# Splitting work moved behind the PSUM reads of each slot, the last output columns in two groups, and TensorE operands at multiples of 256 bytes

## The chip, the core and the metric

The kernel runs on one core of one Trainium2 chip. The metric is the device time of one launch in microseconds (us): the median of three runs is 1772.46 us (1771.05 to 1772.84). TensorE (PE) multiplies, VectorE (DVE) and ScalarE (ACT) work on rows in SBUF and read results out of PSUM, GpSimd (POOL) does small copies and powers, and SyncE (SP) issues all DMAs of this kernel in program order.

## The reference, cut to what matters

One layer of a streaming encoder over 2048 prompt tokens and 64 sample tokens of width 1024, all in float32:

```python
h = rmsnorm(x, norm_in_w) * (1 + scale[:, None]) + shift[:, None]
proj = h @ w_in                         # 1024 -> 7184 columns
b_gate, c_gate, h_a, g_a, z, xbc_raw, dt_raw = jnp.split(proj, idx, axis=-1)
conv_u, new_a = causal_dwconv(c_gate * h_a, buf_a, conv_a_w)
y_a = gated_rmsnorm(b_gate * conv_u, g_a, norm_a_w)
xbc, new_b = causal_dwconv(xbc_raw, buf_b, conv_b_w)   # then + bias, silu
y, s_new = ssd_chunked(xs, dt, a, bs, cs, s0)          # chunked scan, 16 heads, state 128
y_b = gated_rmsnorm(y + d_skip * xs, z, norm_b_w)
out = jnp.concatenate([y_a, y_b], axis=-1) @ w_out     # 2048 -> 1024
return rmsnorm(x + gate[:, None] * out, norm_f_w), new_a, new_b, s_new
```

The outputs are the normalised rows of both sequences and the final states of the two convolutions and of the scan.

## The kernel before, in words

**Split operands.** Every float32 factor of the large products is split into a rounded part `hi` (fp32r) and a rest `lo`, and a product is the sum of three: hi·hi, hi·lo, lo·hi. ACT writes `hi` (a cast), DVE writes `lo` (a subtraction that reads `hi`).

**Projection, `phase_project`.** The tokens go through in two passes: pass 0 takes tokens 0 to 1023, pass 1 tokens 1024 to 2047 and the 64 sample tokens (`PASS`, line 22). The 1024 token columns (1088 in pass 1) and the 1024 rows of the weights are cut in halves, and the four half products of a pair of output tiles are made with seven products (`PRODS`, line 23: A11, S1, S2, S4, S3, A12, A22) in the manner of Strassen and Winograd; S1 to S4 are sums and differences of quarters of `h`. A *group* `g` is one pair of output tiles (256 weight columns), and a *slot* `(g, s)` is one of its seven products: 12 matmuls of 512 columns in pass 0, 24 matmuls of 272 columns in pass 1 (two halves `u` of 12). Groups 0 and 1 are plain products; groups 2 to 27 are pass 0, 28 to 54 pass 1, and 55 is a plain last pair.

**Order inside a slot** (lines 1229 to 1256). Each engine executes its instructions in the order in which they are written: the product on PE (`product`, L276); work put off from the slot before (`run_later`); the weight `hi` of a coming product on ACT (`w_hi`, L242); the *hooks* of that slot; background DVE work (`run_bg`); the weight `lo` on DVE (`w_lo`, L233, with the subtractions that make the Strassen sums of the weights); the read of PSUM (`evac`): for s = 0, 1, 2 an ACT copy into `keep` (L301), for s = 3, 4, 5 a DVE addition (L309), for s = 6 an ACT copy (L307); then the entries of `behind`. Later products accumulate in the same PSUM bank as earlier ones, so slot 2 waits for the read of slot 0, slot 3 for that of slot 1, slot 4 for that of slot 2, slot 6 for that of slot 4, and the first slots of pass 1 for the banks of group 27.

**Between the passes.** The normalised `h` of pass 1 is made during groups 18 to 23 and stored in HBM (`hs_d`). `sums_in(i)` (two calls, for two row halves) loads four quarters into rows 2 to 5; `sums_step(i, n)` (four per call, L849, DVE) makes one of the sums in place and stores it to `hq_d` (L850). They are hooks: `sums_in(0)` in slot (23,6) and its steps in (24,2) to (24,5); `sums_in(1)` in (24,5) and its steps in (25,1) to (25,4). Then `second_in(j, r)` loads the quarter or sum for product `j` into two rows, and `second(j)` splits it into the operand that pass 1 reads: two ACT casts (L171) and two DVE subtractions (L172) of 1088 columns, then the load for `j + 3`. `second(0)`, `(1)`, `(4)`, `(5)`, `(6)` are hooks of slots (27,1), (27,2), (27,6), (28,0), (28,2); `second(2)` and `(3)` stand in `behind` at (27,4) and (27,5).

**Mixing, `phase_mix`.** Sixteen chunks of 128 tokens (and the 64 sample tokens first) go through the scan, both gated norms and the output projection. `out_mm` makes 512 output columns with 24 matmuls (L1430, L1437); `take_b` (L1452 to L1455) scales, multiplies by the gate, adds the residual row on DVE, and sums squares on ACT; `end_rms` makes the factor of the final norm; `scale_out` (L1466) multiplies 1024 columns and stores the row (L1467). For all chunks but the last, the second half of this runs during the next chunk.

**Addresses.** Tiles of a pool are laid one behind the other, each rounded up to 32 bytes per partition; `const`, `stats`, `lp` (later `sp`) are stacked upwards, `hs1`, `hs2`, `hs3` (later `sp1`, `wop`) downwards from the end at 229,344 = 895·256 + 224 bytes. Adding up the sizes: the weights `w0` to `w6` and all operands `hi`, `lo` start 96 bytes past a multiple of 256; `woh`, `wol`, `vah`, `vbh`, `xb` and `state` start 224 past one. In pass 1 a row block of an operand has 2176 bytes, so block k odd starts 128 further, and the half u = 1 another 1088 further. The one exception is group 0 and 1's second token half, `a21`, whose parts lie in row tiles at 160, 192 (hi) and 32, 64 (lo) past a multiple of 256.

Of the kernel before, what the change touches and what calls it, by code (L numbers as in the profile page):

```python
# [27 lines left out]
def kernel(  # L28
# [46 lines left out]
    rbs = const.tile([128, 1], F32, tag="rbs", name="rbs")  # L75
    mhalf = const.tile([128, 1], F32, tag="mhalf", name="mhalf")
    stats = pool(ctx, "stats", bufs=4)

    def ca_w(k, t):
        return par[:, k * 8 + t:k * 8 + t + 1]  # L80
# [20 lines left out]
    def phase_project():  # L101
# [75 lines left out]
            h_tile(q, 544)  # L177
        for i in (0, 1, 6, 7, 2, 3, 4, 5):
            row(i, [128, 1094], f"row{i}_")
        raws = [hs1.tile([128, KT, 256], F32, tag=f"raw{i}", name=f"raw{i}") for i in range(2)]  # L180

        def load_rows(chunks, rows):
            out = []
# [655 lines left out]
        def sums_in(i):  # L839
            for n, (k0, o) in enumerate(((0, 0), (0, 544), (4, 0), (4, 544))):  # L840
                t = row(2 + n, [128, 2, 544], "h_q")
                SP.dma_start(out=t, in_=hs_d[:, k0 + 2 * i:k0 + 2 * i + 2, o:o + 544])
                blocks[n] = t

        def sums_step(i, n):
            a11, a21, a12, a22 = (blocks[x] for x in range(4))
            out, x, y, op = ((a22, a21, a22, ALU.add), (a21, a11, a21, ALU.subtract),
                             (a11, a22, a11, ALU.subtract), (a12, a12, a11, ALU.subtract))[n]
            DVE.tensor_tensor(out=out, in0=x, in1=y, op=op)  # L849
            SP.dma_start(out=hq_d[n, :, 2 * i:2 * i + 2, :], in_=out)  # L850

        for i, t0 in enumerate((23 * 7 + 6, 24 * 7 + 5)):
            hook_at(t0, lambda i=i: sums_in(i))
            for n in range(4):
                hook_at(t0 + 3 + n, lambda i=i, n=n: sums_step(i, n))

        tm = {}
        SOURCE = {"A11": (hs_d, 0, 0), "A12": (hs_d, 4, 0), "A22": (hs_d, 4, 544),
# [17 lines left out]
        hook(26, 0, lambda: second_in(0, 6))  # L876
        hook(26, 1, lambda: second_in(1, 2))
        hook(26, 2, lambda: second_in(2, 4))
        behind = {}
        for j, t, late in ((0, 1, 0), (1, 2, 0), (2, 4, 1), (3, 5, 1), (4, 6, 0), (5, 7, 0), (6, 9, 0)):  # L880
            if late:
                behind[27, t] = lambda j=j: second(j)
            else:
                hook_at(27 * 7 + t, lambda j=j: second(j))

        hook(30, 0, lambda: dt_project(1, 2))
        hook(30, 2, lambda: dt_gather(1))
# [263 lines left out]
        def last_pair():  # L1151
# [16 lines left out]
            fast = [p1.tile([128, 8, 128], F32, tag="lt", name="lt", bufs=2) for _ in range(2)]  # L1168
            p1.tile([128, 8, 128], F32, tag="rb", name="rb_")
            xbs = [p1.tile([128, 8, 128], F32, tag="xb", name="xb", bufs=2) for _ in range(2)]  # L1170
            wop = pool(ctx, "wop", side="right", reuse_waits="tile")
            for k in (0, 1, 2, 3, 4, 5, 7, 8, 9, 10, 11, 12, 13, 14, 15, 6):
                wo[k] = (wop.tile([128, D], F32R, tag=f"woh{k}", name=f"woh{k}"),
# [52 lines left out]
        for g in range(2, last):  # L1226
            p = int(g >= NP0)
            slot_us = 2.75 if p == 0 else 3.05
            for s in range(7):
                now[0] = 7 * g + s  # L1230
                open_banks(p, g, s)
                product(p, g, s)
                run_later()
                if s == 1:
                    w_load(g + 2)
                if s == 2:
                    work[g][1]["begin"](p)
                tg, tj = (g, 6) if s == 0 else (g + 1, s - 1)
                if tg < last:
                    w_hi(tg, tj)  # L1240
                for fn in hooks.get((g, s), ()):
                    fn()
                cost = (W_COST[tj] if tg < last else 0.7) + (0.7 if 3 <= s <= 5 else 0.0) + (0.2 if p and s >= 3 else 0.0)
                credit = min(credit + slot_us - cost, slot_us)
                credit = run_bg(credit)
                if tg < last:
                    w_lo(tg, tj)
                elif s > 0:
                    last_w(s - 1)
                evac(p, g, s)  # L1250
                if (g, s) in behind:
                    behind[g, s]()
                if s == 4:
                    work[g][1]["done"](p, 1)
                if s == 6:
                    work[g][1]["done"](p, 0)
# [36 lines left out]
    def phase_mix():  # L1293
# [156 lines left out]
        def take_b(c, nn, t, ps, r, xr, ss):  # L1450
# [3 lines left out]
            DVE.tensor_tensor(out=xr[:n, s], in0=xr[:n, s], in1=t[:n], op=ALU.add)  # L1454
            ACT.activation(out=t[:n], in_=xr[:n, s], func=AF.Square, accum_out=ss[:n, nn:nn + 1])  # L1455

        def end_rms(c, ss):
            n = ntok(c)
            DVE.tensor_tensor(out=ss[:n, 0:1], in0=ss[:n, 0:1], in1=ss[:n, 1:2], op=ALU.add)
            rf = stats.tile([128, 1], F32, tag="rf", name="rf")  # L1460
            rsqrt_mean(ss[:n, 0:1], n, rf[:n])
            return rf
# [78 lines left out]
        for c in range(16):  # L1541
            n, nxt, nx2 = 128, c + 1, c + 2
            more = nxt < 16
            vb = vb_of.pop(c)
            vbh = split_act(vb, n, "vbh")
            if more:
                prefetch(nxt, 1)
                prefetch_z(nxt, 1)
            if pending:
                pending[0]()  # L1550
            if more:
                va = prefetch_va(nxt)
                ssd1(nxt, 0)
            ra = inv_rms(sqa, n, "ra")
            if pending:
                pending[1]()
            split_dve(vb, n, vbh)
            square(vb, n)
            if pending:
                pending[2]()  # L1560
            sqb = sum_sq(vb, n, "vbh")
            if c == 0:
                SP.dma_start(out=gate, in_=g_d[0].partition_broadcast(128))
            if more:
                xr_next = prefetch_x(nxt)
            if not more:
                store_state()
            pa = out_mm(vah, 0, c, 0)
            if more:
                ssd2(nxt, 0)  # L1570
                decay(nxt, 1)
            t0 = take_a(c, pa, ra)
            if more:
                join1(nxt, 0)
                ssd1(nxt, 1)
                join2(nxt, 0)
                if nx2 < 16:
                    prefetch(nx2, 0)
                    prefetch_z(nx2, 0)
            pa = out_mm(vah, 0, c, 1)  # L1580
            rb_ = inv_rms(sqb, n, "rb")
            if more:
                ssd2(nxt, 1)
            t1 = take_a(c, pa, ra)
            if more:
                vah = split_act(va, n, "vah")
                split_dve(va, n, vah)
                square(va, n)
                join1(nxt, 1)
                sqa = sum_sq(va, n, "vah")  # L1590
                join2(nxt, 1)
                if nx2 < 16:
                    decay(nx2, 0)
            ss = stats.tile([128, 2], F32, tag="fs", name="fs", bufs=2)
            pb0 = out_mm(vbh, 8, c, 0)
            take_b(c, 0, t0, pb0, rb_, xr, ss)
            pb1 = out_mm(vbh, 8, c, 1)

            pending = ends(c, t1, pb1, rb_, xr, ss)
            if more:  # L1600
                xr = xr_next
        for f in pending:
            f()
        stack.close()

    with tc.manual_schedule():
# [30 lines left out]
```

## Time and profile before

| | us |
|---|---|
| median of 3 runs | 1772.46 |
| the profiled execution's own time | 1769.35 |
| its span, first to last instruction | 1767.5 |
| PE busy | 1716.4 (97%) |
| DVE busy | 1306.8 (74%) |
| ACT busy | 826.9 (47%) |
| mean granted TensorE clock | 0.993 |

Where the profile is asked for a stretch, times count from the start of the span. Pass 0 of the Strassen groups begins at 86.0 us, group 24 at 523.98, pass 1 at 606.27; the mixing phase begins after 1215 us. "Idle" behind a row is the time for which that engine had nothing to do before the instruction, and the name behind it is what ended it.

### The profile page before, as it was taken

To read this page: it belongs to the slowest core of one execution; us is meant where nothing else is said; L and a number is where in the kernel's file an instruction comes from. 1 tells how busy PE (TensorE), PEld (TensorE's weight loads), DVE (VectorE), ACT (ScalarE), POOL (GpSimd) and SP (SyncE) were. 2 spreads that over 40 slices of the span, in tenths; PEclk is the share of its full clock that TensorE was granted. 3 is DMA by queue.
4 is the path that set the end of the run, shared out by engine and by line. 5 is a ranking of instruction groups with operands and counts; after the bars stand their busy time and mean duration, and the time that the engine had idled before them with its cause. 6 is when DMAs were issued, how large, how long until landed. Compare 5 with 4: busy or idle time off the path is not lost.

```text
span 1767.5 us, 26974 instructions
## 1 busy us (share of the span) xinstructions
PE 1716.4 (97%) x10561; PEld 1512.3 (86%) x10561; DVE 1306.8 (74%) x2019; ACT 826.9 (47%) x1575; POOL 102.5 (6%) x224
## 2 busy tenths in 40 slices
PE   5999999999999999999999999999899999999997
PEld 4788888887887799999999999999588888888886
DVE  5787779766576646678768767646788888888885
ACT  5644344444653645434333443325455555545551
POOL 0000000000000000001001000000011111101011
PEclk9999999999999999999999999999899999999999
DMA  9222323232548742322322242324653343434341
GB/s 338 72 76 92 96 84 102 89 107 86 170 151 287 248 123 61 91 74 76 113 82 73 74 119 79 113 90 143 213 179 139 137 150 125 160 107 169 108 149 36
DMA packets 186722, 220.20 MB, mean 125 GB/s; under 512 B 21300, under 2 KB 152356, under 8 KB 186596
## 3 DMA queue, kind: packets, MB, share of 16 engines
q1 hardware_dynamic: 186596, 218.49, 38.2%
q8 instruction: 83, 1.36, 0.3%
q14 instruction: 43, 0.35, 0.1%
HBM read 164.31 MB, written 54.15 MB: 124 GB/s over the span
## 4 chain that ended last, share of the span: by engine, by line
PE 86%; DVE 5%; DMA 4%; ACT 3%; issue 2%; SPq 0%; POOL 0%; POOLq 0%; DVEq 0%; ACTq 0%
PE bank L276 54%; PE mm L1430 14%; PE mm L1437 7%; PE sd L1355 2%; PE sd L1359 2%; PE sd L1361 2%; PE sd L1327 1%; DMA h_q<-hs_d 1%; PE sd L1331 1%; DMA praw<-in_w_mod_dram 1%; PE bank L1041 1%; DVE w L233 1%; DMA hq_d<-h_q 0%; DMA xt<-in_x_prompt_dram 0%; PE bank L530 0%
## 5 line engine op out<-in xcount | busy, mean ns | idle before, releaser
L276 PE MATMUL bank<-hiS,w 128*128 128x272 f32 (+1 forms) x2560 | 598.8, 323 | 9.6 <-ACT keep L301 9.5
L276 PEld LDWEIGHTS bank<-hiS,w 128*128 128x128 f32 x2560 | 432.4, 189 | 46.4 <-ACT keep L301 13.0
L276 PE MATMUL bank<-hiA,w 128*128 128x272 f32 (+1 forms) x1920 | 448.9, 322 | 5.8 <-DVE z_row L309 2.4
L276 PE MATMUL bank<-loS,w 128*128 128x272 f32 (+1 forms) x1280 | 412.4, 322 | 0.0
L276 PEld LDWEIGHTS bank<-hiA,w 128*128 128x128 f32 x1920 | 322.8, 188 | 34.7 <-DVE z_row L309 3.3
L233 DVE TENSOR_TENSOR w<-raw,w 128x512 fp32r<-128x512 f32 x318 | 217.9, 688 | 160.0 <-ACT w L242 149.0
L242 ACT CAST w<-raw 128x512 fp32r<-128x512 f32 x318 | 196.1, 622 | 256.7 <-PE bank L276 131.2
L276 PE MATMUL bank<-loA,w 128*128 128x272 f32 (+1 forms) x960 | 308.2, 321 | 0.0
L276 PEld LDWEIGHTS bank<-loS,w 128*128 128x128 f32 x1280 | 242.2, 189 | 15.8
L276 PEld LDWEIGHTS bank<-loA,w 128*128 128x128 f32 x960 | 180.5, 188 | 11.9
L301 ACT COPY keep<-bank 128x272 f32<-128x272 f32 (+1 forms) x240 | 105.9, 450 | 130.7 <-PE bank L276 130.2
L382 DVE SCALAR_TENSOR_TENSOR acc<-raw_row,par,acc 128x1024 f32<-128x1024 f32 (+1 forms) x96 | 126.5, 1318 | 2.0
L233 DVE TENSOR_TENSOR raw<-raw 128x512 f32<-128x512 f32 x161 | 111.0, 690 | 3.7
L1430 PE MATMUL mm<-woh,vbh 128*128 128x512 f32 (+1 forms) x272 | 110.0, 404 | 0.0
L1430 PE MATMUL mm<-woh,vah 128*128 128x512 f32 (+1 forms) x272 | 109.4, 402 | 0.0
L1430 PE MATMUL mm<-wol,vbh 128*128 128x512 f32 (+1 forms) x272 | 106.6, 392 | 0.0
L1430 PE MATMUL mm<-wol,vah 128*128 128x512 f32 (+1 forms) x272 | 106.4, 391 | 0.0
L1289 ACT ACTIVATE lt<-rb,acum 128x128 f32<-128x128 f32 x240 | 73.4, 388 | 3.5 <-DMA rb<-r_d 3.1
L242 ACT CAST w<-t 128x512 fp32r<-128x512 f32 x53 | 32.8, 618 | 74.1 <-PE bank L276 74.1
L1437 PE MATMUL mm<-woh,vbh 128*128 128x512 f32 (+1 forms) x272 | 67.2, 389 | 0.0
L1437 PE MATMUL mm<-woh,vah 128*128 128x512 f32 (+1 forms) x272 | 67.2, 389 | 0.0
L1455 ACT ACTIVATE t<-xr 128x512 f32<-128x512 f32 (+1 forms) x34 | 21.5, 633 | 92.9 <-DVE xr L1454 92.9
(282 smaller groups left out, 2381.8 us busy)
## 6 DMA issues: line engine op xcount, KB each, us to landing
raw<-in_w_in_dram SPq DMA_DIRECT2D x56, 1024.0 KB
xb_d<-acc SPq DMA_DIRECT2D x32, 512.0 KB
xb<-xb_d SPq DMA_DIRECT2D x32, 512.0 KB
rb<-r_d SPq DMA_DIRECT2D x30, 512.0 KB
xt<-in_x_prompt_dram SPq DMA_DIRECT2D x16, 512.0 KB
praw<-in_w_mod_dram SPq DMA_DIRECT2D x16, 512.0 KB
z_d<-z_row SPq DMA_DIRECT2D x16, 512.0 KB
va_d<-c_row SPq DMA_DIRECT2D x16, 512.0 KB
```

The source lines that it names most:

```text
L233: DVE.tensor_tensor(out=out, in0=a, in1=b, op=ALU.subtract)
L242: ACT.copy(out=w[:, 0], in_=w_src(g, j))
L276: PE.matmul(ps[:, 0:n], w[:, a, k, :], h[:, k, o:o + n], start=(s in (0, 1, 5) and k == 0 and i == 0), stop=(k == 3 and i == 2), skip_grou ...
L301: ACT.copy(out=keep[s][:, o:o + n], in_=b["y" if s == 1 else "x"][:, 0:n])
L382: DVE.scalar_tensor_tensor(out=acc[:, 0:n], in0=r[:, k:k + n], scalar=cb_w(k, t), in1=acc[:, 0:n], op0=ALU.mult, op1=ALU.add)
L1289: ACT.activation(out=lt[:, h, :], in_=rb[:, h, :], func=AF.Relu, scale=-1.0, bias=acum[:, c, h0 + h:h0 + h + 1])
L1355: PE.matmul(py4[64 * e:64 * e + 64, j, :], xd[:, 2 * j + e, :], lt[:, 2 * j + e, :], start=True, stop=True)
L1359: PE.matmul(po4[:, j, :], state[:, hf, j * 128:(j + 1) * 128], xb[:, 6 + j // 2, :], start=True, stop=True)
L1361: PE.matmul(ps[:, g * 256:(g + 1) * 256], bc[:, g, :], xe[:, 4 * g:4 * g + 4, :].rearrange("p h q -> p (h q)"), start=True, stop=True)
L1430: PE.matmul(ps[:n], hl[:, 0, k, 0:n], wo[k0 + k][i][:, nn * 512:(nn + 1) * 512], start=(k == 0 and i == 0), stop=False)
L1437: PE.matmul(ps[:n], hl[:, 1, k, 0:n], wo[k0 + k][0][:, nn * 512:(nn + 1) * 512], start=False, stop=(k == 7))
L1455: ACT.activation(out=t[:n], in_=xr[:n, s], func=AF.Square, accum_out=ss[:n, nn:nn + 1])
```

## The change

Four things are edited.

1. `sums_step` runs from `behind` (after the PSUM read of its slot) and no longer as a hook (before the weight `lo` and the PSUM read). The steps of `sums_in(0)` keep their slots (24,2) to (24,5); `sums_in(1)` moves from (24,5) to (24,6), and its steps from (25,1)–(25,4) to (25,4)–(26,0). All seven `second(j)` run from `behind`, in the slots that they had.
2. The last chunk's second half of the output projection goes through `last_out`: columns 0 to 511, then 512 to 767 and 768 to 1023 as groups of their own. The multiplication by the final norm's weight is made per group ahead of the norm's factor; the factor is then applied by DVE to the first 512 columns and by ACT to the two others, and the row is stored in two DMAs.
3. Three unused tiles of 128, 96 and 224 bytes are placed in `lp`, `hs1` and `sp1`. Together with the new 16-byte tile `fl` in `stats`, which takes 32 bytes, they bring `w0` to `w6`, `wdt`, all `hi` and `lo`, `woh`, `wol`, `vah`, `vbh`, `xb`, `state`, `lt`, `xd`, `xe` to multiples of 256; `ident`, `ones` stay 128 past one.
4. The loop over chunks ends with `last_out` in place of its last `pending`.

```diff
+    def pad(p, name, n):
+        p.tile([128, n // 4], F32, tag=name, name=name, bufs=1)
...
+        pad(lp, "pad_l", 128)
         raws = [hs1.tile([128, KT, 256], F32, tag=f"raw{i}", name=f"raw{i}") for i in range(2)]
+        pad(hs1, "pad_h", 96)
...
-                blocks[n] = t
+                blocks[i, n] = t
...
-        for i, t0 in enumerate((23 * 7 + 6, 24 * 7 + 5)):
+        behind = {}
+        def behind_at(t, fn):
+            behind.setdefault((t // 7, t % 7), []).append(fn)
+        for i, (t0, wait) in enumerate(((23 * 7 + 6, 3), (24 * 7 + 6, 5))):
             hook_at(t0, lambda i=i: sums_in(i))
             for n in range(4):
-                hook_at(t0 + 3 + n, lambda i=i, n=n: sums_step(i, n))
+                behind_at(t0 + wait + n, lambda i=i, n=n: sums_step(i, n))
...
-        behind = {}
-        for j, t, late in ((0, 1, 0), (1, 2, 0), (2, 4, 1), (3, 5, 1), (4, 6, 0), (5, 7, 0), (6, 9, 0)):
-            if late:
-                behind[27, t] = lambda j=j: second(j)
-            else:
-                hook_at(27 * 7 + t, lambda j=j: second(j))
+        for j, t in enumerate((1, 2, 4, 5, 6, 7, 9)):
+            behind_at(27 * 7 + t, lambda j=j: second(j))
...
             xbs = [p1.tile([128, 8, 128], F32, tag="xb", name="xb", bufs=2) for _ in range(2)]
+            pad(p1, "pad_p", 224)
...
+        def last_out(c, hl, t0, t1, r, xr):
+            ss = stats.tile([128, 4], F32, tag="fl", name="fl", bufs=1)
+            t2 = sp.tile([128, 4, 64], F32, tag="et", name="t2").rearrange("p a b -> p (a b)")
+            groups = ((0, 512, t0), (512, 256, t1[:, 0:256]), (768, 256, t1[:, 256:512]))
+            for i, (o, w, t) in enumerate(groups):
+                s = slice(o, o + w)
+                ps = bank("mm")
+                for part in range(2):
+                    for k in range(8):
+                        for a in range(2 - part):
+                            PE.matmul(ps[:, 0:w], hl[:, part, k, :], wo[8 + k][a][:, s],
+                                      start=(part == 0 and k == 0 and a == 0), stop=(part == 1 and k == 7))
+                DVE.scalar_tensor_tensor(out=t, in0=ps[:, 0:w], scalar=r, in1=t, op0=ALU.mult, op1=ALU.add)
+                DVE.tensor_tensor(out=t, in0=t, in1=gate[:, s], op=ALU.mult)
+                DVE.tensor_tensor(out=xr[:, s], in0=xr[:, s], in1=t, op=ALU.add)
+                ACT.activation(out=t, in_=xr[:, s], func=AF.Square, accum_out=ss[:, i:i + 1])
+                if i < 2:
+                    DVE.tensor_tensor(out=xr[:, s], in0=xr[:, s], in1=nf[:, s], op=ALU.mult)
+                else:
+                    DVE.tensor_tensor(out=t2, in0=xr[:, s], in1=nf[:, s], op=ALU.mult)
+                if i:
+                    DVE.tensor_tensor(out=ss[:, 0:1], in0=ss[:, 0:1], in1=ss[:, i:i + 1], op=ALU.add)
+            rf = stats.tile([128, 1], F32, tag="rf", name="rf")
+            rsqrt_mean(ss[:, 0:1], 128, rf)
+            y = y_prompt[c * 128:c * 128 + 128, :]
+            DVE.tensor_scalar(out=xr[:, 0:512], in0=xr[:, 0:512], scalar1=rf, scalar2=None, op0=ALU.mult)
+            SP.dma_start(out=y[:, 0:512], in_=xr[:, 0:512])
+            for o, src in ((768, t2), (512, xr[:, 512:768])):
+                ACT.activation(out=xr[:, o:o + 256], in_=src, func=AF.Copy, scale=rf)
+            SP.dma_start(out=y[:, 512:1024], in_=xr[:, 512:1024])
```

More of the change, by code (lines that the diff above doesn't have):

```diff
@@ L842, in sums_in @@
                 SP.dma_start(out=t, in_=hs_d[:, k0 + 2 * i:k0 + 2 * i + 2, o:o + 544])
-                blocks[n] = t
+                blocks[i, n] = t
         def sums_step(i, n):
-            a11, a21, a12, a22 = (blocks[x] for x in range(4))
+            a11, a21, a12, a22 = (blocks[i, x] for x in range(4))
             out, x, y, op = ((a22, a21, a22, ALU.add), (a21, a11, a21, ALU.subtract),
@@ L1250, in phase_project @@
                 evac(p, g, s)
-                if (g, s) in behind:
-                    behind[g, s]()
+                for fn in behind.get((g, s), ()):
+                    fn()
                 if s == 4:
@@ L1593, in phase_mix @@
                     decay(nx2, 0)
+            if not more:
+                last_out(c, vbh, t0, t1, rb_, xr)
+                break
             ss = stats.tile([128, 2], F32, tag="fs", name="fs", bufs=2)
@@ L1599, in phase_mix @@
             pending = ends(c, t1, pb1, rb_, xr, ss)
[L1600 to L1603, printed above, removed]
+            xr = xr_next
         stack.close()
```

## The prediction

> **What bounds the kernel now.** I read the page first, then the chain of waits, then the stretches of groups 24 to 29, then who waited there, and last the end of the span.
>
> ```profile
> span 1767.5 us, 26974 instructions
> PE 1716.4 (97%) x10561; PEld 1512.3 (86%) x10561; DVE 1306.8 (74%) x2019; ACT 826.9 (47%) x1575; POOL 102.5 (6%) x224
> PE 86%; DVE 5%; DMA 4%; ACT 3%; issue 2%; SPq 0%; POOL 0%; POOLq 0%; DVEq 0%; ACTq 0%
> ```
>
> PE sets the end nearly everywhere: a change counts only where PE stands still, where its pace changes, or behind its last matmul. The three edits are one of each kind. The stretches (length, then busy time and instructions of PE, PEld, DVE, ACT, POOL, then the granted clock) are groups 24, 25, 26, 27, 28 and 29:
>
> ```profile
> 523.97:544.28 20.31, 19.33 (x85) 15.70 (x84) 14.95 (x20) 7.34 (x12) 0.00 (x0) 1.00 0.80 287
> 544.28:566.19 21.91, 19.69 (x85) 15.61 (x84) 15.38 (x22) 7.24 (x12) 0.00 (x0) 1.00 0.95 324
> 566.19:585.23 19.04, 19.04 (x85) 15.77 (x84) 10.57 (x16) 8.28 (x13) 0.00 (x0) 1.00 0.88 297
> 585.23:606.26 21.03, 19.40 (x85) 15.69 (x84) 14.25 (x18) 14.95 (x20) 0.00 (x0) 1.00 0.58 187
> 606.26:633.02 26.76, 23.41 (x169) 22.73 (x168) 20.87 (x30) 15.92 (x25) 0.00 (x0) 0.94 0.56 180
> 633.02:654.06 21.04, 21.04 (x170) 21.04 (x169) 9.88 (x18) 9.09 (x18) 0.00 (x0) 1.00 0.36 104
> ```
>
> Groups 26 and 29 run without a stop: 19.04 us for 84 matmuls of 512 columns (2.72 a slot) and 21.04 for 168 of 272 (3.006 a slot). Against these the others lose 1.27, 2.87, 1.99 and 5.72, in all 11.85 us. That is what the first edit can win at most. Who waited (total, times, longest), and the rows of DVE and ACT behind it:
>
> ```profile
> PE bank L276 <- ACT keep L301: 4.0, 3, 1.9
> PE bank L276 <- ACT z_row L307: 2.0, 1, 2.0
> PE bank L276 <- DVE z_row L309: 1.2, 2, 0.9
> PE bank L276 <- DVE b_row L309: 1.0, 1, 1.0
> ...
> 534.08 1.29 DVE L849 TENSOR_TENSOR h_q<-h_q 128x1088 f32<-128x1088 f32 x1 [4.02 <-DMA h_q<-hs_d]
> 538.89 1.29 DVE L849 TENSOR_TENSOR h_q<-h_q 128x1088 f32<-128x1088 f32 x1
> 540.09 0.69 DVE L233 TENSOR_TENSOR w<-raw,w 128x512 fp32r<-128x512 f32 x1
> 540.69 0.69 DVE L309 TENSOR_TENSOR b_row<-bank,keep 128x512 f32<-128x512 f32 x1
> ...
> 552.81 1.29 DVE L849 TENSOR_TENSOR h_q<-h_q 128x1088 f32<-128x1088 f32 x1 [4.82 <-DMA h_q<-hs_d]
> 555.34 0.69 DVE L233 TENSOR_TENSOR raw<-raw 128x512 f32<-128x512 f32 x1
> ...
> 594.75 0.62 ACT L242 CAST w<-raw 128x512 fp32r<-128x512 f32 x1 [3.00 <-DVE raw L233]
> 595.28 2.10 ACT L171 CAST hiS<-t_q 128x1088 fp32r<-128x1088 f32 x2
> 597.28 0.58 ACT L301 COPY keep<-bank 128x512 f32<-128x512 f32 x1
> ...
> 607.32 2.10 ACT L171 CAST hiS<-t_q 128x1088 fp32r<-128x1088 f32 x2
> 609.32 0.57 ACT L307 COPY z_row<-bank 128x512 f32<-128x512 f32 x1
> ```
>
> All stops have one form: a PSUM read that PE needs stands, on its engine, behind a step of the moved kind. At 534.08 and 552.81 DVE has stood for 4.02 and 4.82 us on a load of `h_q`, with weight parts and PSUM reads queued behind; at 597.28 and 609.32 ACT reads PSUM only after two casts of 2.1 us together.
>
> **Edit 1, the moved steps.** Nothing is added or removed: the same 8 DVE steps, 8 stores, 8 loads of `h_q`, and 14 casts, 14 subtractions and the loads that follow them, in another order.
>
> Group 24: the steps keep their slots. DVE still stands until 534.08, now with the weight part and both subtractions of slot 2 done. Then per slot: step 1.20 (538.89 to 540.09 is the pitch of one), weight part 0.60 (540.09 to 540.69), read. The read of slot 4 can start when PE ends that slot, about 537.8; DVE reaches it at 538.3 and is done at 539.0, before (24,6) is due at 540.30 (523.98 + 6·2.72). The 1.27 goes.
>
> Group 25: the loads of `sums_in(1)` are issued one slot later in program order. They wait for the last stores of the first steps, which DVE reaches about 1.3 later than before, and so they land about 1.3 later, near 554. The first step now runs behind the read of (25,4), at about 557: a margin of 3 us. The 2.87 goes. Moved past on SP: `sums_in(1)` stands ahead of the weight load of slot (25,1) as before, and its user comes a group later; the last step falls into (26,0), and its store precedes the loads of `second_in(1)` and `(2)`, which have a group until (27,2). The steps leave DVE about one slot behind at (26,0); it is busy for 10.57 of 19.04 us in group 26 and catches up there.
>
> Groups 27 and 28: with the reads ahead, the waits of (27,4) and of (28,0), whose second half needs the read of 609.32, go, and ACT does its casts in slots where it waited. What remains is DVE's own work. From 589.3 (its first weight part in (27,1)) to the read of (28,3) it must issue 14 subtractions of 1.20, 10 weight parts of 0.60, 7 raw subtractions of 0.72, 3 reads of 0.60 and 2 of 0.45: 30.5 us, and 1.3 us pass until the first cast is there. That ends at 621.1. PE, without stops, wants to begin (28,5), which overwrites that bank, at 585.24 + 7·2.72 + 5·3.006 = 619.3. So 1.8 us stay, and about 0.1 of slow pace after it; 7.71 − 1.9 = 5.8 goes.
>
> Part of group 28's loss is the clock. Its slot after the stop of 2 us ran at 0.63:
>
> ```profile
> 611.60:616.08 4.48, 4.48 (x25) 0.63 0.97 345
> ```
>
> This goes with the stop of (28,0). The stop that stays is no longer than the 1.9 us in group 27, after which that stretch shows 1.00.
>
> Sum: 1.27 + 2.87 + 5.8 = 9.9 us. Bounds: 11.85 (DVE has slack that I don't see) and 0 (each stop returns as another). A loss needs a new stop longer than the old ones; the DVE busy time of groups 27 and 28, 35.1 us, fits into the 40 us that remain, so I exclude more than 1 us.
>
> **Edit 2, the last columns.** The tail of the last chunk:
>
> ```profile
> 1758.47 0.75 DVE L1452 SCALAR_TENSOR_TENSOR t<-mm,rb,t 128x512 f32<-128x512 f32 x1 [3.20 <-PE mm L1437]
> 1759.26 0.69 DVE L1453 TENSOR_TENSOR t<-t,gate 128x512 f32<-128x512 f32 x1
> 1759.98 0.69 DVE L1454 TENSOR_TENSOR xr<-xr,t 128x512 f32<-128x512 f32 x1
> 1760.71 0.63 ACT L1455 ACTIVATE t<-xr 128x512 f32<-128x512 f32 x1 [4.68 <-DVE xr L1454]
> 1761.24 0.19 ACT L1455 ACTIVATION_READ_ACCUMULATOR t<-xr 128x1 f32 x1
> 1761.46 0.16 DVE L1459 TENSOR_TENSOR fs<-fs 128x1 f32<-128x1 f32 x1 [0.79 <-ACT t L1455]
> 1761.89 0.54 POOL L97 TENSOR_TENSOR rf<-ms,mhalf 128x1 f32<-128x1 f32 x1 [13.68 <-DVE ms L96]
> 1762.47 1.28 DVE L1466 SCALAR_TENSOR_TENSOR xr<-xr,rf,nf 128x1024 f32<-128x1024 f32 x1 [0.66 <-POOL rf L97]
> 1763.78 0.34 SPq L1467 DMA_DIRECT2D out_dram<-xr  x1
> ...
> 626.43 0.78 DVE L309 TENSOR_TENSOR z_row<-bank,keep 128x272 f32<-128x272 f32 x2
> L1335 ACT COPY bc<-sd x32: 352/357/373, 1245.0 to 1717.7; 128x256 f32<-128x256 f32 x32
> ```
>
> Before, 5.31 us lie between the last product's first DVE step and the issue of the store. After, the chain is: three DVE steps on 256 columns (0.43 by the nearest row, 0.50 for the first), square 0.36 and its sum 0.19, two small DVE steps, POOL 0.54, two ACT scalings of about 0.4 in a row; with the gaps of the rows 3.85. But the new multiplication by the norm's weight overwrites `xr` and waits for ACT's square of the same columns; behind it in DVE's queue stands the next group. Group 0 takes 0.75 + 0.69 + 0.69 + 0.82 + 0.69 = 3.6 us, a group of 256 columns on PE 2.85: with group 1 the same way, the last group starts 0.6 late. PE itself grows by 24 matmuls; 48 of 256 columns at between 118.6 (the 125.2 of 272 columns less 16 columns) and 125.2 ns are 5.69 to 6.01 us against 5.44. Net: 5.31 − 3.85 − 0.6 − 0.4 = 0.5, and a store of half the bytes lands no later: I take 0.6, bounds 0.2 and 1.5.
>
> **Edit 3, the addresses.** No row of before has a moving operand at a multiple of 256, so this cost is bounded by the nearest rows. A slot of 12 matmuls with operands at 96; one of the `a21` product (160/32 and 192/64 with weights at 96); and the two halves of a slot of pass 1 (12 each, at 96 and 224, then at 160 and 32):
>
> ```profile
> 66.83:69.55 2.72, 2.72 (x13) 1.00 0.00 0
> 69.55:72.33 2.78, 2.78 (x13) 1.00 0.19 35
> 639.03:640.54 1.51, 1.51 (x14) 1.00 1.00 335
> 640.54:642.04 1.50, 1.50 (x14) 1.00 0.58 203
> ```
>
> The address, or the distance of the two operands, moves the pace by 2.2%. In the mixing phase both are at 224, and in the Strassen groups both bases at 96; after, both bases are at 0, and all distances are what they were (0 and 128, 64 and 192 in pass 1). Both 64-byte multiples (192/64) and others (160/32) gave 2.78, so being aligned to 64 alone brings nothing. I take zero. Lower bound: the part of a matmul that doesn't grow with its columns. From 226.67 ns (19.04/84) and 125.2 (21.04/168) a column costs 0.4227 ns and the fixed part is 10.3 ns; over 334 products of 12 and 197 of 24 (182 + 16 and 136; 189 + 8), 8736 matmuls, 90 us. Upper bound: the pace of `a21` everywhere: 334·0.06 + 197·0.066 = 33 us.
>
> The Trainium skill (SBUF — State Buffer, Specifications) gives 16-byte lines as what an access pattern has to respect; every start before is a multiple of 32, so by it the pads bring 0, while the `a21` row shows that this isn't all: by that row the sum could move by 33 us.
>
> **The sum.** 9.9 + 0.6 + 0 = 10.5 us. The profiled execution took 1769.35 and would take 1758.9; it lies 3.1 under the median of the runs, and against that median I forecast 1772.46 − 10.5 = **1762 us**.
>
> **Rivals.**
>
> *New distances or starts slow PE (slower than before).* PE's pace drops to that of the `a21` row wherever it streams split operands: 1762 + 33 = 1795. For: the same engine, data and weights lost 2.2% by addresses alone. Against: the relative placement is kept. It decides from a third of its price on, 10.5 us. Chance 0.13.
>
> *The starts at 256 quicken PE.* Up to the whole fixed part: 1762 − 90 = 1672; half of it 1717. For: the fixed part is there in every row of split operands, none of which starts at 0. Against: it is alike in the two halves of a slot of pass 1, at 96 and 224 and at 160 and 32. The Trainium skill (TensorE: Matmul & The Clock Gate, "Wait — 56ns, not 53.3ns?") gives N/2.4 + 2.5 ns, 215.8 for 512 columns, and has no address in it; by its figure 10.9 ns a matmul lie above it here. Chance 0.16.
>
> *The stops move and don't go.* DVE is the bound in group 28 already and its 5.72 stay: 1762 + 3.8 = 1766; if every stop returns elsewhere, 1762 + 9.9 = 1772. For: DVE's 35.1 us in 40. Against: PE's waits there are for reads that stood in a queue, not for DVE's total. Chance 0.11, of which 0.03 for the last.
>
> *The forecast* has 0.60, with 1757 to 1767 as its own range. Differences under 0.2%, 3.5 us, can't be told from none. Faster: 0.60 + 0.16 + 0.08 = 0.84; same 0.03 + 0.01 of the first rival; slower 0.12. The range takes in the third rival whole, the first up to some 70% of its price and the second to a third of its own: 1730 to 1786, about 0.83.
>
> **What would show it.** Groups 24, 25 and 27 at 19.1 us each and group 28 near 22.9, with one stop on `z_row L309` before (28,5) and no row `h_q` with idle time on a DMA; if group 28 keeps a stop on `z_row L307` or its clock stays under 1.00, the step on ACT is wrong. An undisturbed slot of 12 at 2.72 and group 29 at 21.04: any other value is the addresses, and the forecast falls with it. At the end, the two stores issued within 4.9 us of PE's last matmul, and DVE's first step of the last group starting late.

## The result, and the profile after

The changed kernel took **1759.23 us** (median of 4 runs, 1758.51 to 1761.35) against 1772.05 us (median of 4 runs, 1771.05 to 1772.84) for the kernel before: a ratio of 0.9934, 95% interval 0.9922 to 0.9946, or 12.8 us less. A second set, five runs beside eleven of the kernel before on one chip, gave 1759.73 against 1770.54, a ratio of 0.9935 (0.9923 to 0.9948), or 10.8 us less. The profiled execution took 1758.51 us with a span of 1756.7 us, 10.8 us less than the profiled execution before on both counts. The forecast was 1762, from a gain of 10.5.

The page of the changed kernel, first its span and busy times, then its chain of waits by engine:

```profile
span 1756.7 us, 27034 instructions
PE 1713.1 (98%) x10585; PEld 1511.0 (86%) x10585; DVE 1307.6 (74%) x2026; ACT 828.4 (47%) x1579; POOL 102.9 (6%) x224
PE 89%; DVE 3%; ACT 3%; DMA 2%; issue 2%; SPq 0%; POOL 0%; POOLq 0%; ACTq 0%; DVEq 0%
```

PE has 24 matmuls more than before, and the other engines' counts differ by the few steps of the new tail; in the chain DVE fell from 5% to 3% and DMA from 4% to 2%. The stretches show where the time went. The columns are length, busy time and instructions of PE, PEld, DVE, ACT and POOL, granted clock, DMA share, GB/s; the rows are groups 24 to 29, then an undisturbed slot of pass 0:

```profile
523.88:542.92 19.04, 19.04 (x86) 15.77 (x84) 15.26 (x20) 7.34 (x12) 0.00 (x0) 1.00 0.81 289
542.92:561.96 19.04, 19.04 (x86) 15.77 (x84) 13.64 (x19) 7.39 (x12) 0.00 (x0) 1.00 0.92 301
561.96:581.00 19.04, 19.04 (x86) 15.77 (x84) 12.47 (x18) 8.39 (x13) 0.00 (x0) 1.00 0.98 343
581.00:600.04 19.04, 19.04 (x86) 15.77 (x84) 14.46 (x18) 15.15 (x20) 0.00 (x0) 1.00 0.80 252
600.04:623.31 23.27, 21.58 (x170) 21.14 (x168) 20.45 (x29) 15.33 (x25) 0.00 (x0) 1.00 0.63 205
623.31:644.35 21.04, 21.04 (x170) 21.04 (x169) 9.87 (x18) 9.09 (x18) 0.00 (x0) 1.00 0.34 104
244.97:247.69 2.72, 2.72 (x13) 2.25 (x12) 1.98 (x3) 1.15 (x2) 0.00 (x0) 1.00 0.44 151
```

Groups 24, 25 and 27 now run like group 26, without a stop. Group 28 lost 5.72 us and loses 23.27 − 21.04 = 2.23. Together that is 1.27 + 2.87 + 1.99 + (5.72 − 2.23) = 9.6 us. The pace of undisturbed work, 2.72 a slot and 21.04 in group 29, is to the hundredth what it was.

What PE's products waited for between 523 and 640 us (total, times, longest), where four rows stood before:

```profile
PE bank L282 <- DVE z_row L315: 1.5, 1, 1.5
PE bank L282 <- ACT keep L307: 0.2, 1, 0.2
```

The stop of 1.5 us stands before slot (28,5), and DVE's timeline shows what the read was behind:

```profile
613.69 2.49 DVE L176 TENSOR_TENSOR loA<-t_q,hiA 128x1088 fp32r<-128x1088 f32 x2 [0.28 <-ACT hiA L175]
616.11 0.68 DVE L239 TENSOR_TENSOR w<-raw,w 128x512 fp32r<-128x512 f32 x1
616.71 0.78 DVE L315 TENSOR_TENSOR z_row<-bank,keep 128x272 f32<-128x272 f32 x2
```

The two subtractions of the seventh split, put behind the read of (28,2), occupy DVE until 616.1, then a weight part, and only at 616.71 the read of (28,3) on which PE waits until 617.20.

The other part of the gain is the tail. From the first product of the last output half to the end of the span, the kernel before and then the changed kernel (same columns):

```profile
1747.20:1767.50 20.30, 11.16 (x51) 8.91 (x49) 6.03 (x10) 2.13 (x5) 1.08 (x2) 0.86 0.06 26
```
```profile
1737.62:1756.70 19.08, 11.46 (x75) 10.29 (x73) 7.20 (x17) 3.34 (x9) 1.08 (x2) 0.87 0.07 28
```

That is 1.2 us less, with 0.3 us more on PE. The two terms, 9.6 and 1.2, make up the 10.8 us between the profiles. The changed tail in rows (DVE, then ACT, POOL and SP's stores, from the square of the first column group on):

```profile
1746.46 0.69 DVE L1483 TENSOR_TENSOR xr<-xr,nf 128x512 f32<-128x512 f32 x1 [0.79 <-ACT t L1481]
1747.07 0.48 DVE L1478 SCALAR_TENSOR_TENSOR t<-mm,rb,t 128x256 f32<-128x256 f32 x1
1749.10 0.42 DVE L1483 TENSOR_TENSOR xr<-xr,nf 128x256 f32<-128x256 f32 x1 [0.64 <-ACT t L1481]
1749.51 0.48 DVE L1478 SCALAR_TENSOR_TENSOR t<-mm,rb,t 128x256 f32<-128x256 f32 x1
...
1752.91 0.49 ACT L1494 ACTIVATE xr<-xr,rf 128x256 f32<-128x256 f32 x1
...
1753.01 0.34 SPq L1492 DMA_DIRECT2D out_dram<-xr  x1
1753.45 0.38 SPq L1495 DMA_DIRECT2D out_dram<-xr  x1
```

From the last group's first DVE step (1749.51) to the last store's issue (1753.45) 3.94 us pass, against 5.31 before; the multiplications by the norm's weight wait for ACT's square (idle 0.79 and 0.64) with the next group queued behind them.

### The profile page after: what moved, and what is told of

It reads as the page before. It is cut to its first block, busy times and chain, and to the rows that moved or that the text cites. A ratio compares the mean times of both kernels' runs of the same rounds, so it can differ in the third digit from the quotient of the medians.

```text
span 1756.7 us, 27034 instructions
## 1 busy us (share of the span) xinstructions
PE 1713.1 (98%) x10585; PEld 1511.0 (86%) x10585; DVE 1307.6 (74%) x2026; ACT 828.4 (47%) x1579; POOL 102.9 (6%) x224
## 3 DMA queue, kind: packets, MB, share of 16 engines
q8 instruction: 83, 1.36, 0.3%
## 4 chain that ended last, share of the span: by engine, by line
PE 89%; DVE 3%; ACT 3%; DMA 2%; issue 2%; SPq 0%; POOL 0%; POOLq 0%; ACTq 0%; DVEq 0%
PE bank L282 58%; PE mm L1438 14%; PE mm L1445 7%; PE sd L1363 2%; PE sd L1367 2%; PE sd L1369 2%; DMA praw<-in_w_mod_dram 1%; PE sd L1335 1%; PE sd L1339 1%; PE bank L1048 1%; PE bank L535 0%; PE bank L536 0%; DVE loS L1035 0%; PE bank L826 0%; PE sd L1337 0%
## 5 line engine op out<-in xcount | busy, mean ns | idle before, releaser
L1438 PE MATMUL mm<-woh,vbh 128*128 128x512 f32 (+1 forms) x256 | 103.7, 405 | 0.0
L1438 PE MATMUL mm<-wol,vbh 128*128 128x512 f32 (+1 forms) x256 | 100.5, 392 | 0.0
L1445 PE MATMUL mm<-woh,vbh 128*128 128x512 f32 (+1 forms) x256 | 63.3, 389 | 0.0
L1445 PEld LDWEIGHTS mm<-woh,vah 128*128 128x128 f32 (+1 forms) x272 | 50.2, 185 | 11.5
```

What stands on the lines that cost most here:

```text
L1438: PE.matmul(ps[:n], hl[:, 0, k, 0:n], wo[k0 + k][i][:, nn * 512:(nn + 1) * 512], start=(k == 0 and i == 0), stop=False)
L1445: PE.matmul(ps[:n], hl[:, 1, k, 0:n], wo[k0 + k][0][:, nn * 512:(nn + 1) * 512], start=False, stop=(k == 7))
```

## The experiments

The theory: the stops went because PSUM reads no longer stand behind steps that wait for a load or for casts (9.6 us), the tail brought the rest, and the addresses bring nothing since every distance between the two operands of a product stayed. The rivals: the stops would come back elsewhere when only one kind of step is moved; part of the gain is the new addresses; the distance of the operands is of no account either. Each run is set beside runs of the kernel before on its chip. Their median is 1771.11 us (16 runs) for the sums alone, the splits alone, the tail alone and the change without its unused tiles; 1771.56 (15 runs) for the addresses alone, the tile alone, the other distances and the stop that stayed; 1770.54 (11 runs) for the hooks in new slots, all but the tail and both late steps moved.

**The sums alone.** The kernel before with this part of the change:

```diff
-                hook_at(t0 + 3 + n, lambda i=i, n=n: sums_step(i, n))
+                behind_at(t0 + wait + n, lambda i=i, n=n: sums_step(i, n))
```

> The kernel before with the four sums of each half moved behind the PSUM reads and sums_in(1) one slot later; the splits of the halves of h stay hooks, the tail and the addresses stay. Theory (a read that PE needs stood behind a step that waits for its load): groups 24 and 25 lose nothing, 19.04 us each in place of 20.31 and 21.91, groups 27 and 28 lose what they lost (1.99 and 5.7), and the time is 4.1 us less. Rival (the stops move): a stop of 1 us or more appears in group 25, 26 or 27, and the time is less by at most 2 us.

Measured 1766.15 us, ratio 0.9972 (0.9960 to 0.9983), 5.0 us less. Its stretches, groups 24, 25, 27 and 28 and then slot (28,1):

```profile
524.74:543.77 19.03, 19.03 (x85) 15.77 (x84) 14.66 (x20) 7.34 (x12) 0.00 (x0) 1.00 0.82 288
543.77:562.82 19.05, 19.05 (x86) 15.77 (x85) 14.23 (x19) 7.29 (x12) 0.00 (x0) 1.00 0.91 303
581.86:602.84 20.98, 19.35 (x85) 15.65 (x84) 14.21 (x18) 14.90 (x20) 0.00 (x0) 1.00 0.75 239
602.84:629.66 26.82, 22.18 (x169) 21.30 (x168) 20.90 (x30) 15.98 (x25) 0.00 (x0) 1.00 0.56 179
608.17:612.63 4.46, 3.18 (x26) 2.96 (x24) 2.74 (x5) 2.95 (x5) 0.00 (x0) 1.00 0.99 349
```

Both stops are gone and none took their place: groups 27 and 28 lose 1.94 and 5.78 as before. The last row matters below.

**The splits alone.** The kernel before with all seven `second(j)` in `behind`, in the slots that they had:

```diff
-        for j, t, late in ((0, 1, 0), (1, 2, 0), (2, 4, 1), (3, 5, 1), (4, 6, 0), (5, 7, 0), (6, 9, 0)):
+        for j, t in enumerate((1, 2, 4, 5, 6, 7, 9)):
+            behind_at(27 * 7 + t, lambda j=j: second(j))
```

> The kernel before with all seven splits of groups 27 and 28 behind the PSUM reads, and nothing else. Theory: groups 24 and 25 keep 1.27 and 2.87; groups 27 and 28 together fall from 7.7 us of loss to about 2.2, with one stop left before slot (28,5), and the time is 5.5 us less. Rival (DVE's total sets groups 27 and 28): their loss stays over 5.5 us and the time moves by 2 us at most.

Measured 1766.15 us, ratio 0.9969 (0.9956 to 0.9981), 5.0 us less. Groups 24, 25, 27 and 28:

```profile
524.91:545.19 20.28, 19.33 (x85) 15.69 (x84) 14.98 (x20) 7.34 (x12) 0.00 (x0) 1.00 0.81 288
545.19:567.29 22.10, 19.68 (x86) 15.62 (x84) 15.38 (x22) 7.24 (x12) 0.00 (x0) 1.00 0.96 321
586.33:605.37 19.04, 19.04 (x86) 15.78 (x85) 14.47 (x18) 15.15 (x20) 0.00 (x0) 1.00 0.68 212
605.37:628.66 23.29, 21.59 (x170) 21.16 (x168) 20.46 (x29) 15.33 (x25) 0.00 (x0) 1.00 0.63 202
```

Group 27 loses nothing, group 28 loses 2.25; 24 and 25 keep theirs. The two parts add up: 4.1 and 5.5 us in the stretches.

**Place or time.** The kernel before with the sums in the new slots, but still as hooks, ahead of the weight part and the read:

```diff
-        for i, t0 in enumerate((23 * 7 + 6, 24 * 7 + 5)):
+        for i, (t0, wait) in enumerate(((23 * 7 + 6, 3), (24 * 7 + 6, 5))):
             hook_at(t0, lambda i=i: sums_in(i))
             for n in range(4):
-                hook_at(t0 + 3 + n, lambda i=i, n=n: sums_step(i, n))
+                hook_at(t0 + wait + n, lambda i=i, n=n: sums_step(i, n))
```

> The kernel before with the sums at the slots of the changed kernel (sums_in(1) in (24,6), its steps from (25,4) on), but still as hooks, ahead of each slot's weight part and PSUM read. Theory (it is the place within the slot that counts in group 24, and the later slot in group 25): group 24 keeps its loss of 1.0 to 1.4 us, group 25 loses 0 to 1 us in place of 2.9, 2 to 2.9 us less than before. Rival (the later slot does it all): groups 24 and 25 both at 19.04 us, 4 us less, as with the sums moved behind the reads.

Measured 1765.92 us, ratio 0.9975 (0.9964 to 0.9986), 4.6 us less by the medians, 1.8 by the span. Groups 24 and 25:

```profile
525.83:546.14 20.31, 19.35 (x85) 15.69 (x84) 15.01 (x20) 7.34 (x12) 0.00 (x0) 1.00 0.82 289
546.14:565.18 19.04, 19.04 (x85) 15.77 (x84) 14.90 (x21) 7.39 (x12) 0.00 (x0) 1.00 0.94 318
```

The stretches separate what the medians can't: group 24 keeps its 1.27 us, group 25 loses nothing. In group 24 the place behind the read counts; in group 25 the later slots alone are enough. (That the span gained less than group 25's 2.87 us has a reason outside: pass 0's Strassen groups began 1.8 us later than in the profile before, 87.82 against 86.00.)

**The tail alone, and all but the tail.** First the kernel before with `last_out` only (its small tile in a place that moves no address), then the changed kernel with the old tail, all its tiles kept:

```diff
+            if not more:
+                last_out(c, vbh, t0, t1, rb_, xr)
+                break
```

> The kernel before with the last chunk's second output half in three groups of 512, 256 and 256 columns, and nothing else; no address of an operand of TensorE changes. Theory: from the last group's first DVE step to the last store's issue 3.9 us in place of 5.3, the last group 0.4 to 0.6 late, PE 0.3 to 0.6 longer: in all 0.5 to 0.9 us less, which is within what can be told from no change. Rival (the change after minus the sum of the stops, 12.8 - 10 us, is all here): 2 to 3 us less.

> The changed kernel with the old tail of the last chunk, its tiles and addresses kept. Theory (the tail is worth the 1.1 to 1.2 us between the first product of the last half and the end of the span that the two profiles show): 1.1 us longer than the changed kernel, from the last half's first product to the end 20.3 us in place of 19.1. Rival (the tail gains nothing, as the median of the kernel with the new tail alone has it): the same time as the changed kernel.

The tail alone: 1770.89 us, ratio 1.0002 (0.9993 to 1.0011). All but the tail: 1760.46 us, ratio 0.9936 (0.9924 to 0.9949), beside 1759.73 for the whole change in the same runs. Neither median shows the tail's gain. The stretch from the last half's first product to the end does, for the one and then for the other kernel:

```profile
1748.75:1767.90 19.15, 11.48 (x75) 10.30 (x73) 7.20 (x17) 3.34 (x9) 1.08 (x2) 0.88 0.08 28
```
```profile
1736.04:1756.30 20.26, 11.17 (x51) 8.91 (x49) 6.03 (x10) 2.14 (x5) 1.08 (x2) 0.86 0.06 26
```

It is 19.1 in both kernels with the new tail, 20.3 in both with the old one. Part of what hides it from the medians can be seen at the start of the span. The work ahead of group 2 is the same in all these kernels, and yet the first matmul of that group began at 85.05 us in one profile and at 87.82 in another (all but the tail, then the hooks in new slots):

```profile
85.05 0.39 PE L283 MATMUL bank<-hiA,w 128*128 128x512 f32 x1
```
```profile
87.82 0.39 PE L276 MATMUL bank<-hiA,w 128*128 128x512 f32 x1
```

Even the two profiled executions of the changed kernel itself differ: the first matmul of group 2 at 86.09 and 86.78 us, the spans 1756.7 and 1758.9.

**The addresses alone.** The kernel before with unused tiles of 16, 128, 96 and 224 bytes: all starts as in the changed kernel, in the old order.

```diff
+    pad(stats, "fl", 16)
...
+        pad(lp, "pad_l", 128)
...
+        pad(hs1, "pad_h", 96)
...
+            pad(p1, "pad_p", 224)
```

> The kernel before with unused tiles alone (16, 128, 96 and 224 bytes), in its old order and with its old tail: all operands of TensorE that started at 96 or 224 past a multiple of 256 start at 0, every distance between the two operands of a product is as before. Theory (only the distance counts, not the start): no change, within 3.5 us of before, slots of 12 at 2.72, of 24 at 3.007. Rival (a start at a multiple of 256 is worth the 2.7 us that the change gained beyond its stops and its tail): 2 to 4 us less.

Measured 1771.09 us, ratio 0.9993 (0.9984 to 1.0002): nothing. An undisturbed slot, at starts of 0 in place of 96:

```profile
245.33:248.05 2.72, 2.72 (x13) 2.25 (x12) 1.97 (x3) 1.15 (x2) 0.00 (x0) 1.00 0.40 138
```

**The new tail's tile alone.** The kernel before with one unused tile of 16 bytes, which takes 32 in the lower stack; the weights of the projection then start 128 past a multiple of 256 against operands at 96, the output weights 224 past one against rows at 0:

```diff
+    stats.tile([128, 4], F32, tag="fl", name="fl", bufs=1)
```

> The kernel before with one unused tile of 16 bytes (it takes 32) in the stack of the small statistics, as the new tail needs one, and nothing else; the weights then start 128 past a multiple of 256 against h at 96, the output weights 224 against rows at 0. Theory (distance): slots of 12 at 2.80, 512-column matmuls of the output projection at 233 ns, 20 to 24 us longer than before, less whatever the stops of groups 18 to 27 shrink under a slower PE. Rival (what the changed kernel without pads lost was its order under other addresses): within 3.5 us of before.

Measured **1790.45 us**, ratio 1.0101 (1.0088 to 1.0115), 18.9 us more. An undisturbed slot of pass 0, and group 29; behind them the second output half's matmuls in the kernel before and here (busy time, mean ns):

```profile
249.64:252.44 2.80, 2.80 (x14) 2.26 (x12) 1.91 (x3) 1.10 (x2) 0.00 (x0) 1.00 0.33 105
646.23:667.32 21.09, 21.09 (x171) 21.09 (x169) 9.87 (x18) 9.10 (x18) 0.00 (x0) 1.00 0.35 104
```
```profile
L1437 PE MATMUL mm<-woh,vah 128*128 128x512 f32 x256 | 63.2, 389 | 0.0
```
```profile
L1438 PE MATMUL mm<-woh,vah 128*128 128x512 f32 x256 | 64.9, 396 | 0.0
```

A matmul of 512 columns takes 2.80/12 = 233.3 ns in place of 226.7, and those of the mixing phase lengthen by the same 7 ns; one of 272 columns 21.09/168 = 125.5 in place of 125.2. Over 182 slots of pass 0 at 0.08 us more that is 14.6 us, over pass 1's 189 slots at 0.007 us 1.3, and over some 1600 matmuls of the output projection at 6.7 ns up to 11. That is more than the 18.9 of the medians and the 21.3 between the spans (1788.8 − 1767.5). In the two profiles pass 0 grew by 12.3 us (from 86.00 to 606.27 before, from 87.00 to 619.59 here): in the slots where PE waits anyway a slower pace costs less.

**The change without its three unused tiles.**

```diff
-        pad(lp, "pad_l", 128)
...
-        pad(hs1, "pad_h", 96)
...
-            pad(p1, "pad_p", 224)
```

> The changed kernel without its three unused tiles: the weights then start 128 past a multiple of 256, the split operands of h 96, the operands of the mixing phase 224 (and one stack at 0). Theory (the start address doesn't change PE's pace): as the changed kernel, 12 to 13 us less than before, slots of 12 at 2.72 and of 24 at 3.01. Rival (the distance of the two operands modulo 256 sets the pace, here 32 in place of 0): slots of 12 at up to 2.78, of 24 at up to 3.07, and up to 33 us longer than the changed kernel.

Measured 1781.80 us, ratio 1.0059 (1.0046 to 1.0072): 22.6 us more than the changed kernel's 1759.23, and slower than the kernel before. So the theory put down before it was wrong and the rival held: the tile of the new tail shifts the lower stack by 32 bytes, as above, and the distance of 32 slows PE. A slot of pass 0 and group 29:

```profile
250.22:253.02 2.80, 2.80 (x13) 2.26 (x12) 1.91 (x3) 1.10 (x2) 0.00 (x0) 1.00 0.32 103
637.23:658.33 21.10, 21.10 (x171) 21.10 (x169) 9.88 (x18) 9.10 (x18) 0.00 (x0) 1.00 0.34 104
```

**Distance or odd starts.** In those two kernels some starts were odd multiples of 32. So the changed kernel with other sizes, where all are multiples of 64, at distances of 64 (projection) and 128 (output):

```diff
-        pad(lp, "pad_l", 128)
+        pad(lp, "pad_l", 192)
...
-            pad(p1, "pad_p", 224)
+            pad(p1, "pad_p", 96)
```

> The changed kernel with its unused tiles at 192 and 96 bytes in place of 128 and 224: the weights of the projection start at 64 against h at 0, those of the output projection at 128 against the rows at 0; all are multiples of 64. Theory (a matmul of 512 columns is slow wherever its two operands start at different places modulo 256, as it was at a distance of 32): slots of 12 at 2.80 in place of 2.72, pass 1 the same within 0.3 ns a matmul, 512-column matmuls of the output projection at 233 ns in place of 227, in all 20 to 24 us longer than the changed kernel. Rival (starts at odd multiples of 32 are what was slow): as the changed kernel, 2.72 and 227.

Measured 1782.36 us, ratio 1.0055 (1.0042 to 1.0067): as slow. A slot of pass 0, then a slot of `a21`, whose first six matmuls now have both operands at 64; and the output matmuls:

```profile
250.00:252.80 2.80, 2.80 (x14) 2.26 (x12) 1.91 (x3) 1.10 (x2) 0.00 (x0) 1.00 0.33 110
70.57:73.34 2.77, 2.77 (x13) 2.25 (x12) 2.69 (x5) 1.81 (x4) 0.00 (x0) 1.00 0.37 92
```
```profile
L1445 PE MATMUL mm<-woh,vah 128*128 128x512 f32 x256 | 64.7, 395 | 0.0
```

So it is the distance: both operands at 96 or at 0 gave 226.7 ns, both at 224 gave 227 (14 matmuls of the mixing phase before, from 1699.76 to 1702.94 us), and distances of 32, 64 and 128 about 232 to 233. The `a21` slots show a limit: by their matmuls' start times the six at distance 0 took 1.38 to 1.39 us, where the quick pace would be 1.36; among slow neighbours a few don't reach it. Why the distance counts stays open. So does what it does at 272 columns: in pass 1 the distance changes from one row block to the next in all these kernels, so none of them has a long run at distance 0 there.

**The stop that stayed.** The changed kernel with the seventh split one slot later:

```diff
-        for j, t in enumerate((1, 2, 4, 5, 6, 7, 9)):
+        for j, t in enumerate((1, 2, 4, 5, 6, 7, 10)):
```

> The changed kernel with the seventh split one slot later, behind the read of (28,3) in place of (28,2). Theory (the stop before (28,5) is the read of (28,3) standing in DVE's queue behind the subtractions of that split): group 28 loses 0.4 to 0.8 us in place of 2.2, 1.4 to 1.8 us less than the changed kernel. Rival (DVE's total work is late there, whatever its order): the stop moves to the next slots and group 28 still loses 2 us or more.

Measured 1758.34 us, ratio 0.9920 (0.9906 to 0.9933). Group 28, and DVE around the read that was late:

```profile
600.50:622.55 22.05, 21.57 (x170) 21.16 (x168) 18.92 (x27) 15.22 (x25) 0.00 (x0) 1.00 0.63 199
```
```profile
615.18 0.78 DVE L315 TENSOR_TENSOR z_row<-bank,keep 128x272 f32<-128x272 f32 x2
615.88 2.49 DVE L176 TENSOR_TENSOR loA<-t_q,hiA 128x1088 fp32r<-128x1088 f32 x2
```

Group 28 loses 1.01 us in place of 2.23. The read now stands ahead of the subtractions and comes 2.0 us earlier, counted from the start of its group (615.18 − 600.50 against 616.71 − 600.04). A stop of some 0.4 us turned up one slot later (slot (28,5) took 3.45 us in place of 3.01), so the expected 0.4 to 0.8 was a little too low: the order accounts for most of the stop, and the rival for a part.

**Both late steps moved.** The same, and in the tail the multiplications by the norm's weight of the first two column groups behind the second group's addition:

```diff
-                if i < 2:
-                    DVE.tensor_tensor(out=xr[:, s], in0=xr[:, s], in1=nf[:, s], op=ALU.mult)
-                else:
+                if i == 1:
+                    for o2, w2 in ((0, 512), (512, 256)):
+                        s2 = slice(o2, o2 + w2)
+                        DVE.tensor_tensor(out=xr[:, s2], in0=xr[:, s2], in1=nf[:, s2], op=ALU.mult)
+                elif i == 2:
                     DVE.tensor_tensor(out=t2, in0=xr[:, s], in1=nf[:, s], op=ALU.mult)
```

> The changed kernel with the seventh split behind the read of (28,3), and with the multiplications by the norm's weight of the first two column groups behind the second group's additions. Theory: group 28 loses 1.0 us in place of 2.2, and the last group's first DVE step starts 0.3 us earlier against PE's last matmul: 1.5 us less than the changed kernel. Rival (the multiplications then delay the last group by as much): 1.2 us less, the tail as long as in the changed kernel.

> The changed kernel itself, for a comparison on the same chip: 1759 us, 11 to 13 us less than before.

Measured 1758.23 us (1757.79 to 1758.47), ratio 0.9928 (0.9914 to 0.9942), beside 1759.73 (1758.36 to 1760.66) for the changed kernel, which itself came out 10.8 us under the kernel before, just short of the 11 to 13 expected. Its tail, from the last half's first product to the end, and the last group's first DVE step:

```profile
1737.47:1756.20 18.73, 11.46 (x75) 10.29 (x73) 7.28 (x17) 3.34 (x9) 1.08 (x2) 0.91 0.07 28
```
```profile
1748.97 0.48 DVE L1478 SCALAR_TENSOR_TENSOR t<-mm,rb,t 128x256 f32<-128x256 f32 x1 [0.28 <-PE mm L1476]
```

DVE now waits for PE there (0.28 us) and no longer PE's result for DVE; the tail is 0.35 us shorter, and group 28 gains as in the experiment before. The expected 1.5 us is also the difference of the medians, but these are five runs against five whose ranges touch; the stretches are the better evidence.

## Why the prediction was right, step by step

**The time.** Forecast 1762 from 10.5 us; measured 1759.2 with 12.8 less, and 10.8 less between the profiles and in the second set of runs. The mechanism held, and two terms were off in opposite directions: the splits brought 0.3 less than forecast and the tail 0.6 more, so the traced total of 10.8 lies nearer to 10.5 than its terms do, partly by luck. The further 2 us of the first set's medians are in no stretch and are not explained.

**Groups 24 and 25: 4.14 us.** Right to the hundredth. One indication was wrong, and contradicted the step itself: it said that no row `h_q` would have idle time on a DMA, while the step let DVE stand for the load. The changed kernel has such a row:

```profile
533.74 1.29 DVE L855 TENSOR_TENSOR h_q<-h_q 128x1088 f32<-128x1088 f32 x1 [1.80 <-DMA h_q<-hs_d]
```

DVE still stands there until about 534; the wait is shorter (1.80 for 4.02) mainly because work that used to queue behind it now runs ahead of it. For group 25 the step named the later loads and a margin of 3 us; with hooks in the new slots, that alone removed the loss.

**Groups 27 and 28: 5.8 of 7.71 us.** It was 5.5: 1.99 and 3.49. The step that was mis-sized is "so 1.8 us stay, and about 0.1 of slow pace". 2.23 stayed: one stop of 1.5 before (28,5), in the place foretold, a stop of 0.2 on ACT's `keep`, and some 0.5 of slower pace in the slots around them, where the step had put 0.1. Its reason was only partly right. The step took DVE's 30.5 us of work as what can't be helped; moving one split by one slot, with the same work, took 1.2 of the 2.2 away.

**The clock.** The step "Part of group 28's loss is the clock" was wrong, though it bore no term of its own. The clock did come back to 1.00. But with the sums alone moved, slot (28,1) took 4.46 us at a clock of 1.00 with PE busy for 3.18 of them (the last row there), as long as the 4.48 at 0.63 before. PE would have had to wait for the same read in any case; the slow clock filled that wait and cost nothing. Nor did the stop ahead of it always bring the slow clock. In the profiles of the hooks in new slots and of the addresses alone, which keep that stop, the slot took 4.45 and 4.46 us at 1.00; with the tail alone it took 4.47 at 0.64. Why the clock fell in some and not in others stays open.

**The tail: 0.6 us, measured 1.2,** inside the bounds of 0.2 and 1.5. The chain was sized well (3.85 forecast, 3.94 measured), and PE's growth too (0.4 forecast, 11.46 − 11.16 = 0.3 measured). Two terms were off. The late start was put at 0.6. PE's last matmuls end at 1747.96 + 1.12 = 1749.08, DVE starts at 1749.51, and with the multiplications moved it started 0.04 after PE (1747.81 + 1.12 to 1748.97); so it is 0.4 late:

```profile
1747.96 1.12 PE L1476 MATMUL mm<-woh,vbh 128*128 128x256 f32 x8
```
```profile
1747.81 1.12 PE L1476 MATMUL mm<-woh,vbh 128*128 128x256 f32 x8
```

And a store of half the bytes does land sooner: from its issue to the end of the span 1756.70 − 1753.45 = 3.25 us, before 1767.50 − 1763.78 = 3.72. The tail alone and all but the tail gave 3.3 and 3.7 as well. The step had said "lands no later" and counted nothing; it is worth 0.47. The two stores were issued 3.9 and 4.4 us after PE's last matmul, within the 4.9 named.

**The addresses: 0.** Right, for the reason given: the distances stayed, and the starts alone changed nothing (0.9993). The rival that starts at 256 quicken PE is out: 2.72 a slot at starts of 0. The first rival, that distances slow PE, was the right mechanism for a change that this one isn't; it becomes real without the three unused tiles, at 22.6 us. Its price of 33 us was half as much again too high, since it charged pass 1 with 0.066 us a slot, where 0.007 was measured (21.09 − 21.04 over seven slots). What the prediction didn't see is what the tiles are there for: the 16 bytes of the new tail alone cost the kernel before 18.9 us.

The Trainium skill (SBUF — State Buffer, Specifications) has lines of 16 bytes as the unit that an access pattern should respect; by it neither the pads nor their absence would matter. The measurement decides otherwise: with all starts at multiples of 32 the traces showed up to 6.7 ns a matmul of difference. The Trainium skill (TensorE: Matmul & The Clock Gate, "Wait — 56ns, not 53.3ns?") gives N/2.4 + 2.5 ns, an estimate of 215.8 for 512 columns. The traces don't reach it: no start and no distance tried here came below 226.7 with these operands.

**The rivals on the stops.** None moved elsewhere: each of the two parts alone took away the losses of its own groups, all of 24, 25 and 27 and all but some 2.2 us of 28, and left the other's.

## What to carry to other kernels

In an engine's queue, put first what the bottleneck waits for, then what may itself have to wait; whether a stop comes from the place or from the time is seen when only one of them is changed. Before adding even a 16-byte tile to a stack, work out which operands it shifts against each other: here that was worth more than the whole change. A term of 1 us in 1760 is read from its stretch of the trace, not from medians; between profiles the start alone scattered by more.

## What the runs showed of the hardware that was not expected

- A matmul of 512 fp32r columns took 226.7 ns where moving operand and weights started at the same place modulo 256 bytes, and 232 to 233 at distances of 32, 64 and 128 (up to 2.9%). One of 272 columns took 125.2 to 125.8, with distances mixed in every kernel.
- A granted clock of 0.63 over 4.48 us, behind a stop of 2 us, cost nothing: in other profiles the same slot, behind the same stop, took 4.45 and 4.46 us at full clock, waiting.
- Halving the last store brought the end of the span 0.4 to 0.5 us closer to its issue (3.25 and 3.3 us, against 3.72 and 3.7).
